# A two-layer encoder on one core: expert weights loaded as 16 KB rows for two experts at once, and the next layer's keys and values begun later, through GpSimd's DMA queue

## The chip, the cores and the metric

The kernel runs on one core of a Trainium2 chip. The metric is device time in microseconds (us), from the start of the program to its end. Engines are named as the profile names them: PE (TensorE), ACT (ScalarE), DVE (VectorE), POOL (GpSimd) and SP (SyncE, which here only issues DMAs).

## What is computed

The reference is a trunk of two layers on 512 tokens of width 1024, all in float32. Cut to what matters here:

```
for l in range(2):
    # 1) gated mixing and grouped-query attention from one projection, residual add
    # 2) cross-attention into 256 memory tokens, residual add
    mem_n = rms_norm(mem, mem_norm_g)
    kv = (mem_n @ w_kv[l])            # (256, 1024) x (1024, 2048): keys and values
    # 3) expert choice: 16 experts, each takes its 64 best tokens
    xs = h[idx]                       # (16, 64, 1024)
    a, u = xs @ w_gate[l], xs @ w_up[l]   # per expert 1024 x 1024
    y = (silu(a) * u) @ w_down[l]         # per expert 1024 x 1024
    x = x.at[idx].add(y * gates)
x = rms_norm(x, final_norm_g)
```

## The kernel before

Each layer has a dense part (steps 1 and 2) and an expert part (step 3). The dense part is many small matmuls, three for each product, since each operand is split in a high and a low half (`mm3`, L152 to L154). The expert part goes through the 16 experts in eight pairs (`experts(pr, ...)`), two experts side by side in the two halves of the array. A pair needs 24 MB of weights, for 64 rows of each expert only. Every weight is used once, so this part streams all 16 experts from HBM.

A pair has eight steps, written (pr, i). Steps (pr, 0) to (pr, 3) are gate and up: 512 hidden columns n, then half of the depth k0. Steps (pr, 4) to (pr, 7) are down, in the same way. After each step `between` calls what stands in `todo` and `plan` for it: the ranking of the next pair's tokens, its gather, its transposition and the scattered adds of the pair before. The gather (`gather`, L1188) is an indirect DMA that POOL issues at step 3 of the pair before (one step later in pair 0); its rows are 4168 bytes. PE transposes the gathered tokens at steps 5 and 6 (L1174, `turned`).

The weights are packed in HBM in the order in which they are loaded. A load (`load`, L132) brings 8 KB to each of the 128 partitions, 1 MB in all, from SP's DMA queue. The slots of 8 KB come from several pools, and `order` is a list of slot kinds that is rotated: 14 "w", two "k", two "x" and one "e". A load waits until PE has done its last matmul from the slot's old content. SP takes its loads strictly in the order in which they stand in the program.

Layer 0 has one more task: layer 1's keys and values are worked out during layer 0's expert part. `kv_start` takes slots out of the rotation for the results, for `mT` (the transposed memory tokens) and for the split weights `wkv`. The memory tokens are loaded, scaled on POOL (`mem_scaled`), and transposed on PE in four pieces (`mem_turned`, L346). Then follow eight units u: a load of 1 MB (`kv_load`), its split by ACT and DVE (`kv_split`, L143 and L144) and 48 matmuls (`kv_products`). They stand at numbered steps, `KV_FROM = 2` being pair 2: units end at steps (2, 7), (3, 3), (3, 7), ... (6, 3).

The program is built by a scheduler that may move independent instructions on an engine. Only PE keeps the written order in the down part (`te.strict`).

Of the kernel before, what the change touches and what calls it, by code (L numbers as in the profile page):

```python
# [19 lines left out]
F32 = mybir.dt.float32  # L20
F32R = mybir.dt.float32r
# [7 lines left out]
P = 128  # L29
# [62 lines left out]
def build(tc, a, out, packed):  # L92
# [10 lines left out]
    pair = pool(es, "pair", 2)  # L103
    RD, RM = 3, 14
    kvp = pool(es, "kvp", 2, side="right")
    KV_FROM = 2
    ring, more = [None], [None, None]
    order = deque()
    ps = ent(tc.tile_pool(name="ps", bufs=4, space=PSUM))
# [13 lines left out]
    def slot(shape, dt, nm, hold=False):  # L123
        kind = order.popleft() if order else "w"
        if order and not hold and kind != "y":
            order.append(kind)
        pl, tag = {"w": (ring[0], "w"), "k": (kvp, "k"), "e": (more[0], "e"), "y": (more[1], "y"), "x": (pair, "x")}[kind]
        return pl.tile(shape, dt, name=nm, tag=tag)

    def load(src, b, c):  # L130
        t = slot([P, b, c], F32, "w")
        nc.sync.dma_start(t, src)  # L132
        return t
# [188 lines left out]
    def kv_tiles():  # L322

        while "k" in order:
            order.remove("k")
        return kvp.tile([P, KD, M], F32, name="KT", tag="k"), kvp.tile([P, 2, D], F32, name="V", tag="k")
# [46 lines left out]
    class Final:  # L373
        def __init__(self):
            (a01, self.r), (b01, _) = x_stats(), x_stats()
            self.ssq = [a01[:, 0], a01[:, 1], b01[:, 0], b01[:, 1]]
            o = [slot([P, 2, D], F32, "o") for _ in range(2)]
            self.o = [o[t // 2][:, t % 2] for t in range(TT)]

        def load_gain(self):  # L380
            self.fg = slot([P, D], F32, "fg")
            nc.sync.dma_start(self.fg, a["fg"])
# [24 lines left out]
    for l in range(L):  # L407
# [3 lines left out]
        aTp[0] = pool(dense, f"aT{l}", 2)  # L411
# [401 lines left out]
        wo0 = kvp.tile([P, 4, 512], F32, name="w", tag="k")  # L813
# [37 lines left out]
        order.extend(["w"] * 7 + ["k"] + ["w"] * (RM - 8) + ["k", "w"])  # L851
# [207 lines left out]
        def wload(src, e, k0, c0, cw=512, kw=4):  # L1059
            return load(piece((*src, e), k0, kw, c0, cw), kw, cw)  # L1060

        def first_load(src, k0, c0):

            t = slot([P, 2, 2, 512], F32, "w")
# [5 lines left out]
        def second_load(src, k0, c0):  # L1070

            order.rotate(-1)
            t = again.pop(0)
            for i in range(2):
                k1 = k0 + 2 * i
                nc.sync.dma_start(t[:, i], piece(src, k1, 2, c0, 512))
            return t.rearrange("p i k c -> p (i k) c")

        again = []
# [115 lines left out]
        more[:] = ex1, eyp  # L1195
        order.extend("xxe")
        order.insert(14, "y")
# [7 lines left out]
        if l + 1 < L:  # L1205
            kv = {}

            def kv_start():
                kv["out"] = kv_tiles()
                kv["mT"] = [slot([P, KD, M], F32R, "mT", True) for _ in range(2)]  # L1210
                kv["hi"], kv["lo"] = (slot([P, KD, M], F32R, "wkv", True) for _ in range(2))
                kv["mem"] = load(mem_src, 2, D)

            def kv_load(u):
                kv["w"] = load(piece(("xattn_w_kv", l + 1), 0, KD, u * M, M), KD, M)

            def kv_split(k0):
                for k in range(k0, k0 + 4, 2):
                    split_ps(kv["w"][:, k:k + 2], kv["hi"][:, k:k + 2], kv["lo"][:, k:k + 2])

            def kv_products(u):
                mh, ml = kv["mT"]
                ac = [bank("acc") for _ in range(2)]
                for k in range(KD):
                    wh, wl = kv["hi"][:, k], kv["lo"][:, k]
                    for c in range(2):
                        if u < 4:
                            mm3(ac[c][:, 0:M], wh[:, tsl(c)], wl[:, tsl(c)], mh[:, k], ml[:, k], k == 0, k == KD - 1)
# [8 lines left out]
            step0 = 8 * KV_FROM  # L1237
            planned(step0, kv_start)
            planned(step0 + 1, lambda: mem_scaled(kv["mem"], nc.gpsimd))
            for k2 in range(KD // 2):  # L1240
                planned(step0 + 2 + k2, lambda k2: mem_turned(kv["mem"], kv["mT"], k2), k2)
            for u in range(8):
                planned(step0 + 4 + 4 * u, kv_load, u)
                planned(step0 + 5 + 4 * u, kv_split, 0)
                planned(step0 + 6 + 4 * u, kv_split, 4)
                planned(step0 + 7 + 4 * u, kv_products, u)
        carry = []

        def experts(pr, xT, hT_next, x_next):
# [106 lines left out]
            for n, (c0, cw, chunks) in enumerate(parts):  # L1356
                y = bank("acc")[:, 0:cw]
                for k0, kw in chunks:
                    if last:
                        wd = both_load(wd_, ee, k0, c0, cw, kw)  # L1360
                    else:
                        wd = [second_load((*wd_, ee[e]), k0, c0) if pr == 0 and n == 1 and k0 == 0 else
                              wload(wd_, ee[e], k0, c0, cw, kw) for e in range(2)]
# [21 lines left out]
        for pr in range(NE // 2):  # L1385
            if pr + 1 == NE // 2 and l + 1 < L:
                while "x" in order:
                    order.remove("x")
# [5 lines left out]
        order.clear()  # L1394
        mo.close()
        rst.close()
        if l + 1 < L:
            KT, V = kv["out"]
# [64 lines left out]
```

## Time and profile before

| | |
|---|---|
| device time, median of 3 | 1661.71 us (1660.9 to 1662.37) |
| device time of the profiled execution | 1661.56 us |
| its span, first to last instruction | 1659.8 us |
| PE busy | 1597.8 us, 96% of the span |
| expert part of layer 0 (first to last matmul of L1317) | 383.56 to 867.27 us |
| expert part of layer 1 | 1192.36 to 1644.6 us |
| moved by DMA | 481.89 MB, mean 290 GB/s |

The span is what the prediction counts in; 1.8 us lie around it. The two expert parts are 56% of it. Elsewhere in the span DMA is far from busy.

### The profile page before, as it was taken

Reading aid. Unit: us, or ns where it says so; the run is one execution under the profiler, and the core shown is the slowest. Engines: PE = TensorE matmul, PEld = TensorE weight load, DVE = VectorE, ACT = ScalarE, POOL = GpSimd, SP = SyncE. Lnnn points to the kernel's source line nnn. Section 1 sums busy time; section 2 is a strip of 40 time slices with the busy share of each in tenths; the row PEclk is TensorE's granted clock in tenths of the full one; section 3 lists DMA queues with packets and bytes.
Section 4 is the critical chain, followed back from the end, with each engine's and each line's share of the span. In section 5 each row is a group of like instructions: output and inputs, shape, how many; then the busy total and the mean of one; then the engine's idle time right before and its main releaser. Section 6 shows DMA issues by size and latency. Waiting matters only on the chain.

```text
span 1659.8 us, 21190 instructions
## 1 busy us (share of the span) xinstructions
PE 1597.8 (96%) x8154; PEld 933.8 (56%) x8154; DVE 779.8 (47%) x1836; ACT 511.3 (31%) x1057; POOL 105.2 (6%) x161
## 2 busy tenths in 40 slices
PE   9999999999999999999999999999999999999986
PEld 8667888875334454454448767888633333333333
DVE  5886646534425424423237866663433442332314
ACT  5776545441002111111025784454210000000002
POOL 1100000002010000000002000000300000000000
PEclk9999999999999999999999999999999999999998
DMA  6101342588998999999993102208899999999996
GB/s 223 68 26 55 124 153 77 230 337 303 420 420 359 422 420 420 421 420 420 422 376 102 51 28 100 76 26 355 305 400 420 421 420 421 420 421 421 420 422 272
DMA packets 72837, 481.89 MB, mean 290 GB/s; under 512 B 9248, under 2 KB 9632, under 8 KB 18208
## 3 DMA queue, kind: packets, MB, share of 16 engines
q1 hardware_dynamic: 67792, 468.48, 69.6%
q0 software_dynamic: 2016, 7.47, 1.1%
q10 hardware_dynamic: 2928, 4.59, 0.8%
q8 instruction: 64, 1.05, 0.3%
q14 instruction: 37, 0.30, 0.1%
HBM read 474.14 MB, written 6.37 MB: 290 GB/s over the span
## 4 chain that ended last, share of the span: by engine, by line
PE 64%; DMA 32%; DVE 1%; ACT 1%; issue 1%; POOL 0%; DVEq 0%; SPq 0%; ACTq 0%; POOLq 0%
DMA w<-i_packed 32%; PE acc L1317 19%; PE acc L152 9%; PE acc L153 9%; PE acc L154 9%; PE m L603 2%; PE m L593 2%; PE s L576 1%; PE acc L194 1%; PE s L577 1%; PE s L152 1%; PE s L153 1%; PE s L154 1%; PE m L1304 0%; PE m L870 0%
## 5 line engine op out<-in xcount | busy, mean ns | idle before, releaser
L1317 PE MATMUL acc<-w,xT 128*64 128x512 f32 x2048 | 482.8, 600 | 25.6 <-DMA w<-i_packed 25.1
L1317 PEld LDWEIGHTS acc<-w,xT 128*64 128x64 f32 x2048 | 150.3, 138 | 322.9 <-issue 274.6
L1317 PE MATMUL acc<-w,hT 128*64 128x512 f32 (+1 forms) x1088 | 243.8, 572 | 14.6 <-DVE hT L1294 12.1
L1317 PEld LDWEIGHTS acc<-w,hT 128*64 128x64 f32 x1088 | 79.7, 136 | 141.5 <-issue 110.1
L1285 ACT ACTIVATE hs<-acc,rsl 128x512 f32<-128x512 f32 x32 | 22.0, 687 | 316.4 <-PE acc L1317 271.3
L146 ACT ACTIVATE yhl<-acc,gx 128x512 fp32r<-128x512 f32 (+1 forms) x34 | 22.5, 662 | 300.3 <-PE acc L1317 300.3
L144 DVE TENSOR_TENSOR wl<-w,wh 128x512 fp32r<-128x512 f32 x96 | 66.3, 694 | 93.9 <-ACT wh L143 89.5
L147 DVE SCALAR_TENSOR_TENSOR wl<-w,cols,wh 128x512 fp32r<-128x512 f32 (+1 forms) x96 | 68.9, 727 | 62.3 <-ACT wh L146 54.5
L143 ACT ACTIVATE wh<-w 128x512 fp32r<-128x512 f32 x96 | 60.3, 631 | 106.7 <-PE acc L154 84.7
L1307 DVE TENSOR_TENSOR x<-m,x 128x512 f32<-128x512 f32 (+1 forms) x68 | 44.4, 652 | 86.7 <-PE m L1305 86.7
L146 ACT ACTIVATE wh<-w,cols 128x512 fp32r<-128x512 f32 (+1 forms) x96 | 64.8, 687 | 63.3 <-PE acc L153 37.0
L1307 DVE TENSOR_TENSOR x<-s,x 128x512 f32<-128x512 f32 (+1 forms) x68 | 44.4, 652 | 83.7 <-PE s L1305 83.7
L152 PE MATMUL acc<-wh,ah 128*128 128x512 f32 x192 | 77.8, 406 | 1.0 <-ACT wh L146 0.5
L153 PE MATMUL acc<-wl,ah 128*128 128x512 f32 x192 | 76.8, 400 | 0.6 <-DVE wl L147 0.6
L1286 DVE SCALAR_TENSOR_TENSOR hs<-acc,rsl,hs 128x512 f32<-128x512 f32 x32 | 24.0, 750 | 113.3 <-PE acc L1317 112.9
L154 PE MATMUL acc<-wh,al 128*128 128x512 f32 x192 | 77.0, 403 | 0.0
L584 ACT ACTIVATE P<-s,nb,qsc 128x512 f32<-128x512 f32 x64 | 49.8, 780 | 10.2 <-DVE nb L581 9.5
L147 DVE SCALAR_TENSOR_TENSOR yhl<-acc,gx,yhl 128x512 fp32r<-128x512 f32 (+1 forms) x34 | 24.3, 715 | 58.5 <-ACT yhl L146 58.5
L152 PE MATMUL acc<-wh,oh 128*128 128x512 f32 x128 | 51.5, 403 | 0.0
L1294 DVE COPY hT<-s 128x512 f32<-128x512 f32 x16 | 11.1, 691 | 83.6 <-PE s L1292 83.6
L154 PE MATMUL acc<-ah,wl 128*128 128x512 f32 x128 | 50.2, 392 | 0.0
L154 PE MATMUL acc<-wh,ol 128*128 128x512 f32 x128 | 50.1, 391 | 0.0
(413 smaller groups left out, 2919.2 us busy)
## 6 DMA issues: line engine op xcount, KB each, us to landing
w<-i_packed SPq DMA_DIRECT2D x426, 1024.0 KB, 19.8
w<-i_packed SPq DMA_DIRECT2D x24, 512.0 KB, 7.0
rows<-x ACTq DMA_DIRECT2D x8, 512.0 KB, 2.7
x<-i_x SPq DMA_DIRECT2D x4, 512.0 KB, 5.7
w<-i_mem SPq DMA_DIRECT2D x2, 1024.0 KB, 7.9
o_x<-o SPq DMA_DIRECT2D x4, 512.0 KB, 3.3
rp<-i_rope SPq DMA_DIRECT2D x4, 256.0 KB, 6.4
rows<-i_rows SPq DMA_DIRECT2D x2, 384.0 KB, 6.9
```

Of the source, the lines that this page charges most:

```text
L143: first = nc.scalar.activation(hi, p, AF.Copy)
L144: nc.vector.tensor_tensor(lo, p, hi.bitcast(F32), op=ALU.subtract)
L146: first = nc.scalar.activation(hi, p, AF.Copy, scale=col)
L147: nc.vector.scalar_tensor_tensor(lo, p, col, hi.bitcast(F32), op0=ALU.mult, op1=ALU.subtract)
L152: te(nc.tensor.matmul(o, lh, rh, start=start, stop=False))
L153: te(nc.tensor.matmul(o, lh, rl, start=False, stop=False))
L154: te(nc.tensor.matmul(o, ll, rh, start=False, stop=stop))
L584: last_exp[0] = nc.scalar.activation(pt, s, AF.Exp, bias=nb, scale=qsc[:, t, h:h + 1], accum_out=rs)
L593: last_turn[0] = te(nc.tensor.transpose(p[:, tsl(t)], Ps[t][:, tsl(kt)], ident))
L603: now = te(nc.tensor.matmul(pv[i * 64:(i + 1) * 64], vv[:, kt, kvh * 64:(kvh + 1) * 64], PT[kt], start=kt == 0, stop=kt == TT - 1))
L1307: nc.vector.tensor_tensor(xs_, o, xs_, op=ALU.add)
L1317: te(nc.tensor.matmul(acc[e * 64:(e + 1) * 64], lhs(k)[:, e * 64:(e + 1) * 64], ws[e], start=k == 0, stop=k == KD - 1))
```

## The change

Slots become "doubles" of 16 KB per partition, and one load of 2 MB brings the same chunk of gate, up or down for both experts of a pair. Seven "w" doubles, one "k" and one "x" rotate. Pair 0 still uses pieces of 8 KB, now as halves of doubles (`room`), and the pools "e" and "y" lend a slot for one of its loads each. Keys and values start at step 22, which is (2, 6); units end at steps (3, 7), (4, 3), ... (7, 3). The memory tokens and the eight units' weights are loaded to "e", which has left the rotation, with `nc.gpsimd.dma_start`.

```
-    RD, RM = 3, 14
-    kvp = pool(es, "kvp", 2, side="right")
-    KV_FROM = 2
+    RD, RM = 3, 7
+    kvp = pool(es, "kvp", side="right")
+    KV_STEP = 22
...
+    def double(shape, dt, nm, hold=False):
+        if hold:
+            kind = "w"
+            order.remove(kind)
+        else:
+            kind = order.popleft()
             order.append(kind)
...
-        order.extend(["w"] * 7 + ["k"] + ["w"] * (RM - 8) + ["k", "w"])
+        order.extend(["w"] * RM + ["k"])
...
-        def wload(src, e, k0, c0, cw=512, kw=4):
-            return load(piece((*src, e), k0, kw, c0, cw), kw, cw)
+        def wload(src, ee, k0, c0):
+            t = double([P, 2, 4, 512], F32, "w")
+            nc.sync.dma_start(t, piece(src, k0, 4, c0, 512, ee))
+            return [t[:, i] for i in range(2)]
...
-        more[:] = ex1, eyp
-        order.extend("xxe")
-        order.insert(14, "y")
+        ex_[0] = ex1
+        order.append("x")
+        halves.clear()
...
+            def kv_room(src, *dims):
+                t = ex1.tile([P, *dims], F32, name="w", tag="e")
+                nc.gpsimd.dma_start(t, src)
+                return t
...
-                kv["mT"] = [slot([P, KD, M], F32R, "mT", True) for _ in range(2)]
-                kv["hi"], kv["lo"] = (slot([P, KD, M], F32R, "wkv", True) for _ in range(2))
-                kv["mem"] = load(mem_src, 2, D)
+                for nm in ("mT", "wkv"):
+                    t = double([P, 2, KD, M], F32R, nm, True)
+                    kv[nm] = t[:, 0], t[:, 1]
+                kv["mem"] = kv_room(mem_src, 2, D)
...
-                kv["w"] = load(piece(("xattn_w_kv", l + 1), 0, KD, u * M, M), KD, M)
+                kv["w"] = kv_room(piece(("xattn_w_kv", l + 1), 0, KD, u * M, M), KD, M)
...
-                planned(step0 + 4 + 4 * u, kv_load, u)
-                planned(step0 + 5 + 4 * u, kv_split, 0)
-                planned(step0 + 6 + 4 * u, kv_split, 4)
-                planned(step0 + 7 + 4 * u, kv_products, u)
+                planned(KV_STEP + 6 + 4 * u, kv_load, u)
+                planned(KV_STEP + 7 + 4 * u, kv_split, 0)
+                planned(KV_STEP + 8 + 4 * u, kv_split, 4)
+                planned(KV_STEP + 9 + 4 * u, kv_products, u)
...
-                        pairs = [[wload(src, e, k0, n * 512) for src in (wg_, wu_)] for e in ee]
-                        parts = [(gi, [(k0 + i, [pairs[e][gi][:, i] for e in range(2)]) for i in range(4)])
+                        both = [wload(src, ee, k0, n * 512) for src in (wg_, wu_)]
+                        parts = [(gi, [(k0 + i, [both[gi][e][:, i] for e in range(2)]) for i in range(4)])
```

What the scheduler makes of it is seen at three places. On POOL, in pair 0 of layer 0, this stood before: the iota and the first gather (`xr<-rows`) of the expert part, then the copies from the gathered rows that wait for its landing.

```order
46 L1182 IOTA xr 128x512 [waits DMAHW7_49,PE_49]
47 L1188 DMA xr<-rows_3757,idx 128x1042 [waits DMAHW2_49,DMAHW4_49,DMAHW1_49,DMAHW6_49,DVE_49,Pool_49]
48 L1101 COPY rsl<-xr 128x1 [waits DMASW0_49]
49 L1104 COPY gx<-xr 64x1
50 L1104 COPY gx<-xr 64x1 [waits Pool_49]
```

And this stands there now. The load of the memory tokens (`i_mem`) has moved ahead of the first gather, and their scaling (L359) ahead of the copies. The load's wait on PE is for the last gate and up matmul of pair 0, from slot "e".

```order
46 L1211 IOTA xr 128x512 [waits DMAHW6_49,PE_49]
47 L1240 DMA w<-i_mem 128x2x1024 [waits DMAHW0_49,DVE_49,PE_49]
48 L1217 DMA xr<-rows_3748,idx 128x1042 [waits DMAHW3_49,DMAHW1_49,DMAHW5_49,DVE_49,Pool_49]
49 L359 TENSOR_SCALAR w<-w,rm 128x1024 [waits DMASW0_49]
50 L359 TENSOR_SCALAR w<-w,rm 128x1024
51 L1130 COPY rsl<-xr 128x1 [waits DMASW1_49]
52 L1133 COPY gx<-xr 64x1
```

On SP, this stood before around the loads issued in pair 2 of layer 0. The load w_4861 (second expert of step (2, 4)) takes the slot "e" and waits for PE's gate matmuls of step (2, 1); the five loads behind it wait for no engine.

```order
101 L132 DMA w_4859<-i_packed 128x2048 [waits DMAHW6_49]
102 L132 DMA w_4861<-i_packed 128x2048 [waits DMAHW7_49,PE_49]
103 L132 DMA w_4812<-i_packed 128x2048 [waits DMAHW0_49]
104 L132 DMA w_4814<-i_packed 128x2048 [waits DMAHW1_49]
105 L132 DMA w_4816<-i_packed 128x2048 [waits DMAHW2_49]
106 L132 DMA w_4818<-i_packed 128x2048 [waits DMAHW3_49]
107 L132 DMA w_4887<-i_packed 128x2048 [waits DMAHW4_49]
```

Now that place looks so. The load w_4996 (up of step (3, 2)) takes the double "x" and waits for PE's last down matmul of pair 2, step (2, 7). The load ahead of it, w_4863 (up of step (3, 0)), waits for the gate matmuls of step (2, 2). The four loads behind w_4996 (w_4940 and w_4942 are gate and up of step (3, 1)) wait for no engine.

```order
86 L1081 DMA w_4863<-i_packed 128x4096 [waits DMAHW7_49,PE_49]
87 L1081 DMA w_4996<-i_packed 128x4096 [waits DMAHW5_49,DMAHW0_49,PE_49]
88 L1081 DMA w_4940<-i_packed 128x4096 [waits DMAHW1_49]
89 L1081 DMA w_4942<-i_packed 128x4096 [waits DMAHW2_49]
90 L1081 DMA w_4994<-i_packed 128x4096 [waits DMAHW3_49]
91 L1081 DMA w_5041<-i_packed 128x4096 [waits DMAHW4_49]
92 L1081 DMA w_5043<-i_packed 128x4096 [waits DMAHW6_49,PE_49]
```

On POOL and DVE in pair 3 of layer 0, the first unit's weights now stand so. On POOL their load (`i_packed`) stands behind the copies that wait for the landing of pair 4's gather.

```order
65 L1217 DMA xr<-rows_3748,idx 128x1042 [waits DVE_49,Pool_49]
66 L1130 COPY rsl<-xr 128x1 [waits DMASW4_49]
67 L1133 COPY gx<-xr 64x1
68 L1133 COPY gx<-xr 64x1 [waits Pool_49]
69 L1240 DMA w<-i_packed 128x2048 [waits PE_49]
```

On DVE the first half of that unit's split (`wkv<-w`, which waits for the landing, DMASW5) stands ahead of the copy of `hT` that PE needs for step (3, 5).

```order
677 L165 SCALAR_TENSOR_TENSOR mT<-s,cols,mT 128x256 [waits Activation_49] x2
678 L162 TENSOR_TENSOR wkv<-w,wkv 128x512 [waits DMAHW1_49,DMAHW0_49,DMAHW2_49,DMASW5_49,Activation_49]
679 L162 TENSOR_TENSOR wkv<-w,wkv 128x512 [waits Activation_49]
680 L1329 COPY hT_5099<-m 128x512 [waits PE_49]
681 L162 TENSOR_TENSOR wkv<-w,wkv 128x512 [waits Activation_49] x2
```

## Rows read from the trace of the kernel before

**Rows 1.** The page: busy time, the DMA rate in 40 slices of the span, and the engines of the chain that ended last.
```profile
PE 1597.8 (96%) x8154; PEld 933.8 (56%) x8154; DVE 779.8 (47%) x1836; ACT 511.3 (31%) x1057; POOL 105.2 (6%) x161
...
GB/s 223 68 26 55 124 153 77 230 337 303 420 420 359 422 420 420 421 420 420 422 376 102 51 28 100 76 26 355 305 400 420 421 420 421 420 421 421 420 422 272
...
PE 64%; DMA 32%; DVE 1%; ACT 1%; issue 1%; POOL 0%; DVEq 0%; SPq 0%; ACTq 0%; POOLq 0%
```

**Rows 2.** Stretches of 20 us: busy time and count of each engine, granted PE clock, DMA share, GB/s. Four of layer 0's expert part, then three of layer 1's.
```profile
400.00:420.00 20.00, 20.00 (x94) 6.79 (x92) 6.66 (x20) 3.24 (x4) 0.56 (x1) 1.00 0.96 387
420.00:440.00 20.00, 19.22 (x96) 7.72 (x94) 7.21 (x13) 1.38 (x2) 1.88 (x5) 1.00 1.01 418
500.00:520.00 20.00, 20.00 (x102) 7.22 (x102) 12.08 (x38) 2.71 (x5) 1.02 (x1) 1.00 0.77 312
820.00:840.00 20.00, 16.37 (x73) 5.96 (x71) 1.67 (x3) 0.69 (x1) 0.00 (x0) 1.00 1.01 420
...
1200.00:1220.00 20.00, 20.00 (x96) 7.65 (x96) 10.06 (x34) 4.00 (x6) 1.85 (x6) 1.00 0.94 366
1220.00:1240.00 20.00, 19.22 (x98) 6.80 (x96) 4.49 (x8) 1.37 (x2) 1.60 (x2) 1.00 1.01 421
1620.00:1640.00 20.00, 19.22 (x106) 8.44 (x104) 4.68 (x7) 3.95 (x9) 0.00 (x0) 1.00 0.99 406
```

**Rows 3.** What SP's queue waited for from 478 to 512 us (us in total, times, longest).
```profile
SPq L132 <- PE acc L1317: 23.1, 4, 19.6
```

**Rows 4.** DMA share in tenths from 500 to 512 us, in slices of 0.3 us.
```profile
DMA  1411000000000000990679999999999999999999
```

**Rows 5.** PE in time order (start, us, what), a pair without keys and values: pair 2 of layer 1 and the first matmul of pair 3.
```profile
1299.29 7.04 PE L1317 MATMUL acc<-w,xT 128*64 128x512 f32 x32
...
1324.55 7.03 PE L1317 MATMUL acc<-w,xT 128*64 128x512 f32 x32
1336.39 3.65 PE L1317 MATMUL acc<-w,hT 128*64 128x512 f32 x16 [0.78 <-DVE hT L1294]
...
1350.12 2.31 PE L1317 MATMUL acc<-w,xT 128*64 128x512 f32 x10
```

**Rows 6.** PE in pairs 2 and 3 of layer 0: one piece of `mem_turned`, the last step of pair 2, gate and up of step (3, 3), the first matmul of a unit of keys and values and the next weight matmul behind the unit.
```profile
515.79 0.66 PE L346 MATMUL s<-ident,w 128*128 128x128 f32 x4
516.38 7.09 PE L1317 MATMUL acc<-w,xT 128*64 128x512 f32 x32
...
540.24 3.65 PE L1317 MATMUL acc<-w,hT 128*64 128x512 f32 x16
...
577.41 1.02 PE L1317 MATMUL acc<-w,xT 128*64 128x512 f32 x2
...
585.87 0.39 PE L152 MATMUL acc<-mT,wkv 128*128 128x256 f32 x1
...
591.80 3.65 PE L1317 MATMUL acc<-w,hT 128*64 128x512 f32 x16
```

**Rows 7.** POOL around the first gather of layer 0 (start, us, what, idle before it and what ended that), then PE at its use. The second row is DVE's, at the end of pair 0's gate and up matmuls.
```profile
418.59 0.56 POOL L1182 IOTA xr<- 128x512 f32 x1 [25.53 <-PE acc L1317]
...
420.33 0.75 DVE L1286 SCALAR_TENSOR_TENSOR hs<-acc,rsl,hs 128x512 f32<-128x512 f32 x1 [6.41 <-PE acc L1317]
...
423.74 1.17 POOL L1188 DMA_INDIRECT xr<-rows,idx  x1 [4.59 <-DVE idx L1187]
432.55 0.18 POOL L1101 COPY rsl<-xr 128x1 f32<-128x1 f32 x1 [7.65 <-DMA xr<-rows,idx]
...
434.63 0.40 PE L1305 MATMUL s<-yhl,oS 128*128 128x512 f32 x1
434.86 0.60 PE L1174 MATMUL m<-ident,xr 128*128 128x128 f32 x4
...
439.56 0.65 PE L1317 MATMUL acc<-w,xT 128*64 128x512 f32 x2
```

**Rows 8.** DMA queues (packets, MB, share of 16 engines) while the gather of Rows 7 moves (q0 is POOL's queue, q1 SP's): from 428 to 428.9 us, its first packets, and from 428 to 432 us, nearly all of it. No q0 packet lies before 428.
```profile
q1 hardware_dynamic: 32, 0.25, 68.4%
q0 software_dynamic: 29, 0.12, 33.3%
...
q1 hardware_dynamic: 154, 1.13, 69.1%
q0 software_dynamic: 142, 0.53, 33.5%
```

**Rows 9.** SP's queue alone: from 600 to 640 us, all rows of 8 KB (261 of the packets are semaphores), and from 850 to 860 us, rows of 4 KB but for a few (105 semaphores).
```profile
DMA packets 2316, 16.85 MB, mean 421 GB/s; under 512 B 261, under 2 KB 261, under 8 KB 261
q1 hardware_dynamic: 2314, 16.82, 101.1%
...
DMA packets 880, 3.75 MB, mean 375 GB/s; under 512 B 105, under 2 KB 105, under 8 KB 740
q1 hardware_dynamic: 880, 3.75, 92.6%
```

**Rows 10.** POOL at pair 4's gather (issue, and the copies at its landing), then DVE: a unit's four splits in a row and the copy of `hT`.
```profile
580.11 0.98 POOL L1188 DMA_INDIRECT xr<-rows,idx  x1 [39.10 <-DVE idx L1187]
589.49 0.18 POOL L1101 COPY rsl<-xr 128x1 f32<-128x1 f32 x1 [8.40 <-DMA xr<-rows,idx]
589.62 0.42 POOL L1104 COPY gx<-xr 64x1 f32<-64x1 f32 x2
...
590.85 2.52 DVE L144 TENSOR_TENSOR wkv<-w,wkv 128x512 fp32r<-128x512 f32 x4 [4.05 <-ACT wkv L143]
596.08 0.69 DVE L1294 COPY hT<-m 128x512 f32<-128x512 f32 x1 [2.71 <-PE m L1292]
```

**Rows 11.** The chain of waits in layer 1's expert part, its last piece before the loads take it over, by time.
```profile
1273.88 6.92 PE acc L1317 x32
...
1281.67 20.38 DMA w<-i_packed
```

**Rows 12.** PE at the end of layer 0's expert part: the last down products.
```profile
861.44 2.81 PE L1317 MATMUL acc<-w,hT 128*64 128x256 f32 x24
...
865.32 1.95 PE L1317 MATMUL acc<-w,hT 128*64 128x256 f32 x16
```

**Rows 13.** The DMA issues from 527.68 to 527.70 us: the last load of step (3, 0), its count, size and time from issue to landing.
```profile
w<-i_packed SPq DMA_DIRECT2D x1, 1024.0 KB, 21.3
```

More of the change, by code (lines that the diff above doesn't have):

```diff
@@ L121, in bank2, with room, shaped @@
         return bank("ms"[turn[0]])
-    def slot(shape, dt, nm, hold=False):
-        kind = order.popleft() if order else "w"
-        if order and not hold and kind != "y":
+    def double(shape, dt, nm, hold=False):
[4 more added lines that the diff above has]
+            kind = order.popleft()
             order.append(kind)
-        pl, tag = {"w": (ring[0], "w"), "k": (kvp, "k"), "e": (more[0], "e"), "y": (more[1], "y"), "x": (pair, "x")}[kind]
+        pl, tag = {"w": (ring[0], "w"), "k": (kvp, "k"), "x": (pair, "x")}[kind]
         return pl.tile(shape, dt, name=nm, tag=tag)
+    def room(*dims):
+        if not order:
+            return ring[0].tile([P, *dims], F32, name="w", tag="w")
+        if not halves:
+            t = double([P, 2, 2048], F32, "w")
+            halves.extend((t[:, 0], t[:, 1]))
+        return shaped(halves.pop(0), dims)
+    def shaped(v, dims):
+        v = v[:, 0:math.prod(dims)]
+        names = "abc"[:len(dims)]
+        return v.rearrange(f"p ({' '.join(names)}) -> p {' '.join(names)}", **dict(zip(names, dims)))
     def load(src, b, c):
-        t = slot([P, b, c], F32, "w")
+        t = room(b, c)
         nc.sync.dma_start(t, src)
@@ L322, in kv_tiles @@
     def kv_tiles():
[L324 removed]
+        if "k" in order:
             order.remove("k")
[L326 removed]
+        t = kvp.tile([P, 2, 2048], F32, name="KV", tag="k")
+        return shaped(t[:, 0], (KD, M)), shaped(t[:, 1], (2, D)), shaped(t[:, 0], (4, 512))
     rm = base.tile([P, 2], F32, name="rm")
@@ L376, in __init__ @@
             self.ssq = [a01[:, 0], a01[:, 1], b01[:, 0], b01[:, 1]]
-            o = [slot([P, 2, D], F32, "o") for _ in range(2)]
-            self.o = [o[t // 2][:, t % 2] for t in range(TT)]
+            o = double([P, TT, D], F32, "o")
+            self.o = [o[:, t] for t in range(TT)]
         def load_gain(self):
-            self.fg = slot([P, D], F32, "fg")
+            self.fg = room(D)
             nc.sync.dma_start(self.fg, a["fg"])
@@ L1068, in first_load, with second_load @@
             return t
-        def second_load(src, k0, c0):
+        def second_load():
             order.rotate(-1)
[L1073 to L1079, printed above, removed]
+            for e in range(2):
+                for i in range(2):
+                    nc.sync.dma_start(again[e][:, i], piece((*wd_, e), 2 * i, 2, 512, 512))
+            return [t.rearrange("p i k c -> p (i k) c") for t in again]
         def both_load(src, ee, k0, c0, cw, kw):
-            t = slot([P, 2, kw, cw], F32, "w")
+            t = room(2, kw, cw)
             nc.sync.dma_start(t, piece(src, k0, kw, c0, cw, ee))
@@ L1361, in experts @@
                     else:
-                        wd = [second_load((*wd_, ee[e]), k0, c0) if pr == 0 and n == 1 and k0 == 0 else
-                              wload(wd_, ee[e], k0, c0, cw, kw) for e in range(2)]
+                        wd = (ahead2[k0] if pr == 0 and n == 0 else second_load() if pr == 0 and k0 == 0 else
+                              wload(wd_, ee, k0, c0))
                     weights([(k, [wd[e][:, k - k0] for e in range(2)]) for k in range(k0, k0 + kw)], y,
@@ L1386, in build @@
             if pr + 1 == NE // 2 and l + 1 < L:
-                while "x" in order:
-                    order.remove("x")
+                order.remove("x")
                 hT_next, x_next = [aT_pair("a")], x_stats()
@@ L1394, in build @@
         order.clear()
+        halves.clear()
         mo.close()
@@ L1397, in build @@
         if l + 1 < L:
-            KT, V = kv["out"]
+            KT, V, wo0 = kv["out"]
     es.close()
```

37 lines of the change are left out of this document (23 added, 14 removed).

## The prediction

> **What bounds the kernel now.** The page first: PE is busy for 96% of the span, yet the chain that ended last runs 32% over weight loads [rows 1]. These are shares over stages with different limits, so the stages are read apart. In the dense parts DMA moves 23 to 155 GB/s in most slices, and only PE counts. In the expert parts DMA stands at 420 GB/s for many slices on end. The stretches of 20 us show where it does not [rows 2]: at the start of each expert part (387 and 366 GB/s, all slots full), and once in the middle of layer 0, at 500 (312). There SP stood 19.6 us at one load that waited for PE [rows 3], and DMA ran dry from 501.2 to 504.8 us, and was at full rate from about 506 [rows 4]. Afterwards it is saturated to the layer's end. In layer 1 the chain goes over to the loads at 1281.67 [rows 11] and DMA is full from 1220 to 1640 [rows 2]. So a part's end is the end of its bytes, where PE keeps up. PE's own price of a pair is 1350.12 - 1299.29 = 50.8 us [rows 5]; 24 loads at 421.2 MB per ms [rows 9] are 24 x 1.0486 / 0.4212 = 59.7 us, 2.49 each. With two units of keys and values, 591.80 - 585.87 = 5.9 us each [rows 6], PE needs 62.7 us. In layer 0's later pairs PE and DMA are level, and a wait on either one shows.
>
> **Where layer 0 restarts.** Pair 1 begins at 439.56 [rows 7]; two pairs without keys and values end at 439.6 + 2 x 50.8 - 0.4 = 540.8 us. Call this T; before, it was 543.8, since pieces of mem_turned lay in pair 2 [rows 6]. In the new order SP stands at w_4996 until T, with four loads behind it whose slots are free. This head-of-line wait is what was worth some 5 us at 500, moved and not removed. All loads up to step (3, 0) are out by then. The last of them landed at 527.7 + 21.3 = 549.0 [rows 13]; take away the old gap, 4.7 us [rows 4], and one unit's load that is no longer ahead of it, 2.5, and DMA is done with them at about 541.8, or up to 2 us later because a double is released as late as its second half. With T = 540.8 there is hardly a gap; with a later T there is one, and every us of T is a us of the layer. So nothing that DMA gains or loses before T counts in layer 0.
>
> **T itself.** POOL now issues the memory tokens ahead of the first gather, on the same queue. The old gather landed just before 432.55 and PE's add before its use ended at 434.86, so it has about 2.1 us to spare [rows 7]. The two queues share one row each, by turns: 32 packets of SP's against 29 of POOL's in the first 0.9 us, 154 against 142 in all [rows 8]. That is two on each of the 16 engines, so the turns are of one row. In busy time, rows of 4 KB move 3.75 / (10 x 0.926) = 405 MB per ms and rows of 8 KB 16.82 / (40 x 1.011) = 416 [rows 9]: a row takes 16 x 4.096 / 405 = 0.16 us and 0.315 us. Each doubling halves a row's fixed part, so after the 2.7% from 4 to 8 KB I take 1.4% from 8 to 16: about 0.62 us a row (estimate). The memory tokens are 16 rows of 4 KB per engine: 16 x (0.16 + 0.62) = 12.5 us. They are issued at about 420.3, when DVE too sees the last gate and up matmul [rows 7]. The gather's first packet came 4.4 us after its issue [rows 7, 8]; a plain load may start sooner, 2 us at least. Then the gather, 8 x (0.16 + 0.62) = 6.2 us. It lands between 420.3 + 2 + 18.7 = 441.0 and 443.4, against 434.7 at which PE wants it: PE stands 6.3 to 8.7 us; I take 7, since a plain load has no list of rows to read first. If the turns were by bytes it would be nothing. So T = 547.8, bounds 540.8 and 549.5. The Trainium skill ("DMA: Bandwidth & Descriptors", Queues, rings and completion order) has an engine drain a whole packet of 9 to 17 descriptors from one queue before it switches; rows 8 disagree, with two of each queue on every engine in 0.9 us. By its rule the order would be 8 rows of SP's, the tokens, 8 of SP's, the gather: 424.7 + 5.0 + 2.6 + 5.0 + 1.3 = 438.6, a stand of 4 us in place of 7.
>
> **After T, PE's side.** The restart: the first data come 2.3 us after T, w_4996 first although it is wanted last, then gate of (3, 1) at T + 12. PE has step (3, 0) and the add until T + 10, so it loses 3 us (0 to 5). Then the first unit. Gate and up of (3, 3) begin at T + 0.4 + 25.3 + 3 + 3 x 0.6 (three pieces of mem_turned) = T + 30.5 [rows 5, 6]. Pair 4's gather is issued 580.1 - 577.4 = 2.7 us later, lands 9.4 us behind that [rows 6, 10], and 2.4 later still beside rows of 16 KB; its copies take 0.6. Only then POOL issues the unit's weights: T + 45.6. Start 2 to 4.4, and 8 x (0.31 + 0.62) = 7.4: landed at T + 55 to 57.4. ACT's first split and two of DVE's (2.52 / 4 each) and the copy of hT, 0.7, follow [rows 10]: T + 57.5 to 60. Step (3, 5) needs that copy 1336.39 - 1324.55 = 11.8 us after (3, 3) began [rows 5], with the fourth piece T + 43. PE stands 14.5 to 17; with turns by bytes 10. I take 15. Later units load a whole unit's time ahead of use, so their loads are costed at nothing; their cover is about 31 us. The rest is work: pair 3 is 50.8 + 5.9 + 2.4 = 59.1, pairs 4 to 6 are 3 x 62.7 = 188.1, pair 7 about 50 + 5.9 (less ranking, one unit that was not there). To the last weight product: T + 0.4 + 59.1 + 188.1 + 55.9 + 3 + 15 = T + 321.5.
>
> **After T, DMA's side.** 108 loads' worth in doubles, 8 of pair 7's down, 8 units: 124 x 2.49 = 308.7 us, four gathers 5.0. Doubles gain 1.4% by rows 9; bounds 0 (a row may be cut in two on the way) and 2%. That is 54 x 4.98 x 1.4% = 3.8 us. Last landing T + 2.3 + 309.9 = T + 312.2, and the last products are 867.3 - 861.4 = 5.9 behind [rows 12]: T + 318. PE sets the end: 547.8 + 321.5 = 869.3 against 867.3, **+2.0 us** in layer 0. The slower parts of mem_scaled, SP's fewer issues and the later w_o load of the dense part hide behind PE, and are costed at nothing.
>
> **Layer 1.** No keys and values, no wait out of order on SP. About 80 doubles lie behind 1220: 80 x 4.98 x 1.4% = 5.6 us gained, bounds 0 and 8. Coarser release at the start delays saturation by half a double at most: 2 us lost. The gather beside longer rows comes 2.4 us later and PE has 2; but PE is not what ends this part. **-3.6 us.**
>
> **Sum.** 1661.56 + 2.0 - 3.6 = 1660.0 us; the profiled execution lies 0.15 under the median, so the forecast for the median is 1660.1.
>
> **The rivals.** (a) The memory tokens do not delay the gather, because the turns are by bytes or the load is early enough: T = 540.8, layer 0 at 862.3, 7 us better than the forecast: 1653. Rows 8 speak against it, but the rows of before never have two transfers in POOL's queue. (a') The two queues change turns by groups of 8 rows, as the Trainium skill's page above has it: 4 us instead of 7, so 1657. Rows 8 give it little. (b) Slower: a row of 16 KB moves no byte faster. Then layer 0 ends by DMA at T + 321.8 and, level with PE, a little above, 870; layer 1 is +2: 1666. It decides once the gain is under 0.25%. Rows 9 give a gain between 4 and 8 KB only. (c) Also slower: POOL's loads start later than a gather does. The Trainium skill ("SBUF — State Buffer", the trap box on DVE blocking DMA) says that descriptors written on GpSimd wait while DVE holds the shared port, which speaks against this queue; no row here isolates it. As a mechanism of this kernel: DVE begins its work at 420.33 too [rows 7]. Each us later at the gather and at the first unit adds a us: with 3 and 3, 1666. (d) A row of 16 KB goes as two of 8 KB: then no gain, but the gather lands at 436, 1.5 us late, and the unit's stall is 12: 1661.
>
> **Chances.** Forecast, together with (d), 0.40; (a) 0.27; (a') 0.05; (b) 0.15; (c) 0.08; other losses 0.05. What a measurement of this kernel tells from no change is about 0.2%, 3.3 us: faster 0.34 (some of the forecast's lower edge), same 0.38, slower 0.28. The forecast's own range is 1656 to 1664. With (a) and (b) and one us of their own bounds, 1651 to 1669.
>
> **What would show it.** Right: POOL's wait for the first gather ends near 442, PE's first L1205 of pair 0 stands 6 to 8 us, SP stands some 30 us at one load in pair 2 and DMA dips near 545 to 550, PE waits about 15 us for hT in pair 3, layer 1 is 3 to 4 us shorter. Wrong: two packets of SP's queue in place of one per row, a gather in time, PE waiting for loads rather than hT, or layer 1 not shorter.

## The result, and the profile after

The changed kernel takes **1671.53 us** (median; 1671.0 to 1671.61) against 1661.81: a ratio of 1.0058, 95% interval 1.0041 to 1.0076. It is 9.7 us **slower**, outside the stated range. The profiled execution takes 1671.54 us, its span is 1669.7.

The stages tell where. Layer 0's expert part, first to last weight product, went from 483.7 us (383.56 to 867.27) to 500.2 (383.09 to 883.24): +16.4. Layer 1's went from 452.2 to 447.4 (1208.03 to 1655.40): -4.9. The rest gave back 1.7.

The page after: busy time, DMA rate in 40 slices, the chain that ended last [rows 1].

```profile
PE 1575.7 (94%) x8154; PEld 923.9 (55%) x8154; DVE 781.7 (47%) x1836; ACT 513.4 (31%) x1057; POOL 110.4 (7%) x170
...
GB/s 215 73 26 52 125 127 101 195 381 306 360 425 427 315 426 414 426 426 427 426 322 177 54 26 76 77 50 241 344 372 427 427 426 426 427 428 426 426 428 288
...
PE 77%; DMA 18%; DVE 2%; ACT 1%; issue 1%; POOL 0%; SPq 0%; DVEq 0%; ACTq 0%; POOLq 0%
```

Where DMA is full it now moves 425 to 428 GB/s, not 420 to 422. The chain has moved from the loads to PE, although PE is busy for less of the span. So PE waits, and mostly for things that are not the weights. What PE waited for in layer 0's expert part (us, times, longest):

```profile
PE acc L1352 <- DVE hT L1329: 21.5, 8, 16.0
PE m L1203 <- DMA xr<-rows,idx: 9.4, 1, 9.4
PE acc L1352 <- DMA w<-i_packed: 5.1, 2, 2.6
```

The first gather, on POOL and then at PE [rows 7]:

```profile
420.10 0.96 POOL L1240 DMA_DIRECT2D w<-i_mem  x1 [1.40 <-PE acc L1352]
423.27 1.04 POOL L1217 DMA_INDIRECT xr<-rows,idx  x1 [2.21 <-DVE idx L1216]
437.17 5.69 POOL L359 TENSOR_SCALAR w<-w,rm 128x1024 f32<-128x1024 f32 x2 [12.86 <-DMA w<-i_mem]
443.88 0.19 POOL L1130 COPY rsl<-xr 128x1 f32<-128x1 f32 x1 [1.02 <-DMA xr<-rows,idx]
...
443.96 1.09 PE L1203 MATMUL m<-ident,xr 128*128 128x128 f32 x4 [9.37 <-DMA xr<-rows,idx]
444.98 5.35 PE L1352 MATMUL acc<-w,hT 128*64 128x512 f32 x16
...
450.85 1.51 PE L1352 MATMUL acc<-w,xT 128*64 128x512 f32 x6
```

The gather lands at 443.8, not 432.5, and PE stands 9.37 us. Then PE is slow (the columns are start and us): the four transpositions take 1.09 us instead of 0.60, the 16 products of a down step 5.35 instead of some 3.65. The stretches of 2 us show the reason, in the column before the DMA share, the granted clock:

```profile
436.00:438.00 2.00, 0.00 (x0) 0.00 (x0) 0.00 (x0) 0.00 (x0) 0.83 (x1) 1.00 1.04 436
...
440.00:442.00 2.00, 0.00 (x0) 0.00 (x0) 0.00 (x0) 0.00 (x0) 2.00 (x2) 0.50 1.08 450
...
446.00:448.00 2.00, 2.00 (x8) 0.58 (x6) 0.00 (x0) 0.00 (x0) 0.00 (x0) 0.50 0.08 33
448.00:450.00 2.00, 2.00 (x10) 0.42 (x6) 0.00 (x0) 0.00 (x0) 0.00 (x0) 0.89 0.00 0
450.00:452.00 2.00, 2.00 (x12) 0.91 (x12) 1.05 (x2) 0.69 (x1) 0.56 (x1) 1.00 0.54 106
```

PE did nothing from 434.6 to 443.96. The clock fell to 0.50, the level of 1.2 GHz, in this stand and was back at 1.00 (2.4 GHz) only between 448 and 450, more than 4 us after PE worked again. Pair 1 begins at 450.85 instead of 439.56. The stand costs DMA time as well: SP's next load waits for PE until 450.38, and DMA runs dry, some 5 us from 446 to 454.

SP's waits from 440 to 580 us, and stretches of 20 us (the first: SP issued w_4996 only at 552.9; the second: layer 1, DMA full):

```profile
SPq L1081 <- PE acc L1352: 107.6, 21, 17.6
SPq L1081 <- DMA w<-i_packed: 24.9, 3, 12.5
...
540.00:560.00 20.00, 20.00 (x96) 7.65 (x93) 5.18 (x8) 1.38 (x2) 1.05 (x4) 1.00 0.50 194
...
1500.00:1520.00 20.00, 15.61 (x76) 5.27 (x74) 3.05 (x6) 0.69 (x1) 0.97 (x1) 1.00 1.01 426
```

The two longest waits are both at w_4996, 12.5 us for a landing and then 17.6 for PE: the 30 us in all that the prediction named. Ten us of DMA are lost in the first stretch, against 4.7 before [rows 4]. Pair 3, on PE, POOL and DVE [rows 5, 6, 10]:

```profile
565.60 3.65 PE L1352 MATMUL acc<-w,xT 128*64 128x512 f32 x16 [2.50 <-DMA w<-i_packed]
571.82 5.08 PE L1352 MATMUL acc<-w,xT 128*64 128x512 f32 x16 [2.57 <-DMA w<-i_packed]
...
614.45 5.94 PE L1352 MATMUL acc<-w,hT 128*64 128x512 f32 x16 [16.02 <-DVE hT L1329]
...
588.88 0.96 POOL L1217 DMA_INDIRECT xr<-rows,idx  x1 [38.91 <-DVE idx L1216]
599.80 0.18 POOL L1130 COPY rsl<-xr 128x1 f32<-128x1 f32 x1 [9.96 <-DMA xr<-rows,idx]
600.28 0.58 POOL L1240 DMA_DIRECT2D w<-i_packed  x1
...
612.50 1.29 DVE L162 TENSOR_TENSOR wkv<-w,wkv 128x512 fp32r<-128x512 f32 x2 [16.19 <-ACT wkv L161]
613.72 0.68 DVE L1329 COPY hT<-m 128x512 f32<-128x512 f32 x1
```

PE waits twice for loads that SP held back, then 16.02 us for hT, which stands on DVE behind a split that waits for the unit's load, issued only at 600.28. The steps behind the second and third wait take 5.08 and 5.94 us instead of 3.65.

### The profile page after: what moved, and what is told of

The parts are those of the page before. It is cut to its first block, busy times and chain, and to the rows that moved or that the text cites. A ratio compares the mean times of both kernels' runs of the same rounds, so it can differ in the third digit from the quotient of the medians.

```text
span 1669.7 us, 20871 instructions
## 1 busy us (share of the span) xinstructions
PE 1575.7 (94%) x8154; PEld 923.9 (55%) x8154; DVE 781.7 (47%) x1836; ACT 513.4 (31%) x1057; POOL 110.4 (7%) x170
## 4 chain that ended last, share of the span: by engine, by line
PE 77%; DMA 18%; DVE 2%; ACT 1%; issue 1%; POOL 0%; SPq 0%; DVEq 0%; ACTq 0%; POOLq 0%
PE acc L1352 29%; DMA w<-i_packed 16%; PE acc L170 10%; PE acc L171 10%; PE acc L172 10%; DMA xr<-rows,idx 2%; PE m L623 2%; PE m L613 2%; PE s L596 1%; PE acc L212 1%; PE s L597 1%; PE s L170 1%; PE s L171 1%; PE s L172 1%; PE s L1339 1%
## 5 line engine op out<-in xcount | busy, mean ns | idle before, releaser
L1352 PE MATMUL acc<-w,xT 128*64 128x512 f32 x2048 | 461.9, 596 | 24.7 <-DMA w<-i_packed 24.1
L1352 PEld LDWEIGHTS acc<-w,xT 128*64 128x64 f32 x2048 | 144.0, 137 | 307.1 <-issue 267.7
L1352 PE MATMUL acc<-w,hT 128*64 128x512 f32 (+1 forms) x1088 | 239.0, 583 | 38.8 <-DVE hT L1329 25.4
L1352 PEld LDWEIGHTS acc<-w,hT 128*64 128x64 f32 x1088 | 76.2, 139 | 167.0 <-issue 126.2
L162 DVE TENSOR_TENSOR wl<-w,wh 128x512 fp32r<-128x512 f32 x88 | 60.8, 694 | 85.7 <-ACT wh L161 83.3
L161 ACT ACTIVATE wh<-w 128x512 fp32r<-128x512 f32 x88 | 55.2, 631 | 97.4 <-PE acc L172 81.0
L170 PE MATMUL acc<-wh,a 128*128 128x512 f32 x192 | 77.8, 406 | 1.0 <-ACT wh L164 0.5
L171 PE MATMUL acc<-wl,a 128*128 128x512 f32 x192 | 76.8, 400 | 0.6 <-DVE wl L165 0.6
L172 PE MATMUL acc<-wh,a 128*128 128x512 f32 x192 | 77.0, 403 | 0.0
L170 PE MATMUL acc<-wh,o 128*128 128x512 f32 x128 | 51.5, 402 | 0.0
L172 PE MATMUL acc<-wh,o 128*128 128x512 f32 x128 | 50.0, 391 | 0.0
L171 PE MATMUL acc<-wl,o 128*128 128x512 f32 x128 | 50.0, 391 | 0.0
```

Source lines behind the costliest of these rows:

```text
L161: first = nc.scalar.activation(hi, p, AF.Copy)
L162: nc.vector.tensor_tensor(lo, p, hi.bitcast(F32), op=ALU.subtract)
L170: te(nc.tensor.matmul(o, lh, rh, start=start, stop=False))
L171: te(nc.tensor.matmul(o, lh, rl, start=False, stop=False))
L172: te(nc.tensor.matmul(o, ll, rh, start=False, stop=stop))
L1352: te(nc.tensor.matmul(acc[e * 64:(e + 1) * 64], lhs(k)[:, e * 64:(e + 1) * 64], ws[e], start=k == 0, stop=k == KD - 1))
```

## The experiments

Theory A is that of the prediction, with the clock added: layer 0 lost its 16 us by three stands of PE (waits in which it does nothing) that come from the order on POOL, DVE and SP. Theory B: the late keys and values, and slots released in 16 KB, cost it. Theory C is about the gain in layer 1: not the length of a row, but fewer and larger issues. Each of the times below stands beside the kernel before on the same chip, 1661.6 to 1662.6 us.

**Memory tokens behind the gather.** One scheduling dependency (the lines that keep the two handles are left out, here and below):

```
...
+                nosync(last_d[0], last_g[0], "behind the gather")   # the memory tokens' load behind the last gather
```

> The changed kernel with one more scheduling dependency: the load of the memory tokens stands on POOL behind the gather that is written just before it (pair 3's) and no longer ahead of pair 1's. Theory A (the 16 us lost in layer 0 are stands of PE caused by the order on POOL and SP, and the lower clock behind them): the first gather lands near 433 us, PE's stand of 9.4 us in pair 0 and the half clock behind it (2.2 us) are gone, pair 1 begins near 439.5 instead of 450.9, and since SP's blocked load is released 11 us earlier the wait for loads in pair 3 shrinks from 5 us to under 2. Total 1657 us (1654 to 1661). Rival B (layer 0 is longer because a unit of keys and values now lies in pair 7 and doubles are released late): what PE gains in pair 0 is waited for later, total above 1667 us.

Measured: 1659.12 us, ratio to before 0.9987 (0.9977 to 0.9996): 12.4 us less than the changed kernel. What PE waited for:

```profile
PE acc L1354 <- DVE hT L1331: 22.7, 8, 17.2
PE acc L1354 <- DMA w<-i_packed: 4.1, 3, 2.6
PE m L1204 <- DMA xr<-rows,idx: 0.4, 1, 0.4
```

The first stand is gone (0.4) and pair 1 begins at 440.38. B falls as the main cause. The waits for loads shrank by only 1 us, though, where under 2 us in all were expected: SP still stands at w_4996, until 542.3, and the DMA share is 0.90 from 520 to 540 and 0.84 from 540 to 560.

**Splits behind the add.** The first unit's splits, one step later and behind the down product's split:

```
+                        nosync(hi, last_y[0], "behind the scatter")
+                        nosync(lows[0], last_y[1], "behind the scatter")
...
+                planned(KV_STEP + 7 + 4 * u + (u == 0), kv_split, 0, u == 0)
+                planned(KV_STEP + 8 + 4 * u, kv_split, 4, u == 0)
```

> The changed kernel, but the first unit's splits stand on ACT and DVE behind the split of pair 3's first down product, so that hT does not queue behind a load. Theory A: the stand of 16 us at step (3, 5) is gone; PE reaches the unit itself at about the time its weights land and stands there 2 to 5 us; PE gains 12 to 15 us in pair 3. DMA has been full since 555 us and its last landing (869.8) lets layer 0 end no earlier than 875.7 against 882.9, so the total gains 7 to 10 us: 1663 us (1660 to 1666). Rival B: PE is not what ends layer 0, total above 1668 us.

Measured: 1666.65 us, ratio 1.0032 (1.0019 to 1.0044), a gain of 4.9 us, less than expected. The stand moved:

```profile
PE acc L1357 <- DMA w<-i_packed: 8.3, 6, 2.6
PE m L1204 <- DVE x L1347: 6.9, 1, 6.9
PE acc L1357 <- DVE hT L1333: 6.3, 8, 0.8
```

hT costs nothing beyond its usual 0.8 each. But the splits, which still wait for the load, now hold DVE's adds of the same pair back, 6.9 us, and PE waits 3 us more for loads later. The right place was missed by one more instruction.

**SP in written order.** Each load of a double depends on the one written before it:

```
+            d = nc.sync.dma_start(t, piece(src, k0, 4, c0, 512, ee))
+            if last_w:
+                nosync(d, last_w.pop(), "in order")
+            last_w.append(d)
```

> The changed kernel with SP's loads of doubles kept in the order in which they are written, so that the load for slot x in pair 3 stands behind the three that have free slots. Theory A: no run dry of DMA at 540 to 553 us (share 0.50 in the stretch 540 to 560 becomes above 0.9), PE does not wait at step (3, 1) (5 us and 1.4 us of lower clock saved), but the two stands for POOL's transfers stay. Total 1665 us (1662 to 1668). Rival: the dry time is hidden under the later stand at (3, 5), since DMA catches up while PE stands: total within 2 us of 1671.5.

Measured: 1664.29 us, ratio 1.0015 (1.0006 to 1.0025), a gain of 7.2. The same stretch as above, and no wait of PE for a load in layer 0:

```profile
540.00:560.00 20.00, 20.00 (x95) 8.27 (x92) 5.95 (x10) 1.37 (x2) 0.77 (x3) 1.00 1.01 429
```

**Rows of 8 KB.** Each load of 2 MB becomes two:

```
+            v = piece(src, k0, 4, c0, 512, ee)
+            for i in range(2):
+                nc.sync.dma_start(t[:, i], v[:, i])
```

> The changed kernel, but each load of 2 MB issued as two of 1 MB, rows of 8 KB as before; slots, order and POOL unchanged. Theory A (rows of 16 KB move 1.5% faster, and POOL's queue gets one of its rows per row of SP's): DMA at 421 GB/s instead of 427, layer 1 loses its 5.8 us; but the memory tokens and the gather behind them move beside shorter rows, the gather lands near 437 instead of 443.8, PE stands 2 to 3 us and keeps its clock, the second stand is 3 us shorter. Total 1667 us (1663 to 1671). Rival C (the higher rate comes from 2 MB per issue, or the turns are by bytes): rate 427 stays or the first stand stays 9 us, total 1671 us or more.

Measured: 1667.32 us, ratio 1.0036 (1.0022 to 1.005). Layer 1's part is 453.2 us again, at 418 GB/s in the stretch in which the changed kernel has 426; PE's stand at the first gather falls to 2.0:

```profile
1500.00:1520.00 20.00, 16.11 (x76) 5.60 (x77) 3.74 (x7) 0.69 (x1) 1.45 (x4) 1.00 1.01 418
...
PE m L1205 <- DMA xr<-rows,idx: 2.0, 1, 2.0
```

Both halves of A's claim on rows hold: DMA moves less with the shorter row, and the longer row delays whoever takes turns with it. The edit also makes two issues of each, though, so by the rate alone C is not out; the second run with rows of 8 KB, below, tells the two apart.

**All three orders.** The first three edits together.

> The three orders together in the changed kernel: memory tokens behind pair 3's gather, the first unit's splits behind pair 3's first down product, SP's doubles in written order. Theory A: all three stands of PE in layer 0 go or shrink (first 0.4 us, wait for loads in pair 3 none, third at most 9 us with its clock), DMA is full from about 425 us on with no dry stretch, and layer 0 ends by DMA at about 859 us against 867.3 before and 882.9 in the changed kernel; layer 1 keeps 447 us against 452 before. Total 1649 us (1645 to 1654), faster than both kernels. Rival B (a late unit of keys and values, or doubles, cost layer 0 more than the stands did): total above 1658 us.

Measured: **1648.55 us**, ratio 0.9927 (0.991 to 0.9943): faster than both kernels, 13 us under before. Layer 0's part is 478.0 us, layer 1's 447.3. DMA is full from 420 to 840. What is left is the stand behind the splits, with its clock:

```profile
580.00:600.00 20.00, 11.89 (x52) 5.02 (x54) 7.04 (x12) 2.88 (x5) 2.09 (x6) 0.85 1.00 424
...
PE m L1209 <- DVE x L1353: 7.5, 1, 7.5
```

**The unit's load ahead of the gather.** SP in written order, the memory tokens behind pair 2's gather and transposed two steps earlier, and the first unit loaded two steps earlier. The splits' order is not in it; they stand where the scheduler puts them:

```
+            planned(12, kv_mem)
+            planned(KV_STEP - 2, kv_start)
...
+                planned(KV_STEP + 6 + 4 * u - 2 * (u == 0), kv_load, u)
```

> Like the kernel with all three orders, but the memory tokens are loaded behind pair 2's gather, transposed two steps earlier, and the first unit's load stands on POOL ahead of pair 4's gather, so that it lands long before hT is copied (its splits are where the scheduler puts them). Theory A: PE has no stand above 1 us in pairs 0 to 3 and keeps its clock. DMA ends layer 0 as in the kernel with all three orders, so the total is the same or up to 3 us better: 1647 us (1643 to 1652). Rival: it is PE's third stand that ends layer 0 there, and this one is 5 us or more better than that one.

Measured: 1649.27 us, ratio 0.9925 (0.9908 to 0.9941), the same time as with all three orders. No long stand is left; PE instead waits 13 times for loads, and layer 0's part is 478.0 us here too:

```profile
PE acc L1361 <- DMA w<-i_packed: 12.6, 13, 1.8
```

So with DMA full, the third stand costs nothing; it costs where DMA has lost time as well.

**Rows of 8 KB in all three orders.** As above, to see what a row is worth where DMA ends a stage.

> The kernel with all three orders, but each load of 2 MB issued as two with rows of 8 KB. Theory A (rows of 16 KB move 1.5% faster): layer 1 loses 5 us; layer 0, where PE and DMA end within a few us of each other, loses 3 to 5. Total 1657 us (1654 to 1660). Rival C (the doubles help by fewer issues and waits, not by row length): under 1651 us.

Measured: 1661.36 us, ratio 0.9995 (0.9985 to 1.0004). Layer 0's part is 483.7 us (478.0 with rows of 16 KB) and layer 1's 453.3 (447.3): 11.6 us in the two, more than expected; C would have the total under 1651. (The two totals differ by 12.8 us, but the kernel before ran 1 us longer on this run's chip.)

This edit too changes the length of a row and the number of issues together; the single packets tell which counts. From 1300 to 1400 us, with the engines full in either case, a row of 16 KB took 616 ns on average and a row of 8 KB 314 to 315, so two short rows take 12 to 13 ns more, 2%. What an issue adds on each engine, a packet of 4 bytes for its semaphore, took 9 ns: 0.36% of the engines' time with rows of 8 KB, 0.18% with 16 KB. So nearly all of the gain lies in the rows, as A has it, and the fewer issues give some 0.2%. No run changes the one without the other.

**Keys and values late in the kernel before.** `step0` is 6 more, and units two steps later still, as in the changed kernel:

```
-            step0 = 8 * KV_FROM
+            step0 = 8 * KV_FROM + 6
...
```

> The kernel before (rows and slots of 8 KB, all loads on SP) with keys and values at the steps of the changed kernel: start at step 22, units end at (3, 7) to (7, 3). Theory A: the later steps by themselves cost little, since DMA ends layer 0 there: 1662 us (1659 to 1665). Rival B: the unit in pair 7 and the fuller pairs make PE the end of layer 0: 1667 us or more.

Measured: 1667.79 us, ratio 1.0047 (1.0029 to 1.0064): 6.2 us slower, as B expected. PE at the end of pair 7's up, at the unit, and at the layer's last products [rows 12]:

```profile
844.67 2.31 PE L1317 MATMUL acc<-w,xT 128*64 128x512 f32 x8
846.91 0.38 PE L152 MATMUL acc<-wkv,mT 128*128 128x256 f32 x1
...
872.04 1.95 PE L1317 MATMUL acc<-w,hT 128*64 128x256 f32 x16
```

Pair 7 begins at 810.35 (810.01 before) and is paced by loads until its up ends at 847; then come the unit, 5.9 us, and the whole down part, 21 us, which is PE's own. Before, the down part began at 845.3 at once. So a unit in the last pair shows in full, even where DMA sets the pace. That the changed kernel pays this is not shown: behind pair 3 its PE waits for no load, so that a unit is PE's work in whichever pair it stands.

**Keys and values from ACT's queue.**

```
-                nc.gpsimd.dma_start(t, src)
+                nc.scalar.dma_start(t, src)
```

> The changed kernel with the loads of the memory tokens and of the eight units issued from ACT's queue instead of POOL's; SP's order as in the changed kernel. Theory A (the gather waits because it is second in POOL's own queue, and the first unit's load because it is issued behind POOL's wait for a landing): the first gather moves beside the memory tokens and lands at 434 to 436 us, PE stands at most 1.5 us and keeps its clock; the first unit's load is issued some 6 us earlier, so the stand for hT falls from 16 us to 7 to 10; the dry stretch of SP's order remains. Total 1656 us (1652 to 1660). Rival (any load beside 16 KB rows of SP's queue is this slow, whoever issues it): stands and total as in the changed kernel, above 1667 us.

Measured: 1657.81 us, ratio 0.9971 (0.9959 to 0.9982). PE's waits:

```profile
PE acc L1352 <- DVE hT L1329: 15.1, 8, 9.6
PE acc L1352 <- DMA w<-i_packed: 6.6, 4, 2.6
PE m L1203 <- DMA xr<-rows,idx: 2.1, 1, 2.1
```

The gather lands at 435.96, beside the memory tokens instead of behind them, and PE stands 2.1 us. The wait for hT is 6.4 us shorter, as expected of a load that does not stand behind POOL's wait. The clock still fell once: it was 0.50 from 438 to 440, and the down step behind the 2.1 us took 5.35 us, not 3.65. Behind the 2.0 us in the run with rows of 8 KB it stayed at 1.00.

**PE kept busy in its stand.** Dummy products on an unused accumulator, ahead of the transposition that waits:

```
+                    for _ in range(60):      # 38 in the second run
+                        te(nc.tensor.matmul(p[:, 0:P], ident, ident, start=True, stop=True))
```

> The changed kernel with 60 dummy matmuls of 128 columns (0.145 us each, 8.7 us in all, written to an unused accumulator) on PE just ahead of the transposition that waits for the first gather. Theory A: the half clock at 439 to 449 us follows from PE having nothing to do in its stand; with the dummies the granted clock stays at 1.0, the down step behind the stand takes 3.06 us instead of 4.8, pair 1 begins 2 us earlier, total 1669.5 us (1668 to 1671). Rival: the clock falls for another reason, step and total unchanged at 1671.5 us or later by what the dummies overrun.

Measured: 1672.74 us, ratio 1.0065 (1.0049 to 1.0082). A dummy took 0.226 us, not 0.145: the 60 products stand in the profile as 120 instructions, where a transposition is one. So they lasted 13.6 us and overran the gather by 4.4; but the clock stayed at 1.00 and the down step took 3.65 us. Hence the shorter run:

> As the run with dummy matmuls, with 38 instead of 60: at the 0.226 us that one took there they last 8.6 us and end before the gather lands. Theory A: the clock stays at 1.0, the down step behind the stand takes 3.06 us instead of 4.8 and the transposition ahead of it 0.6 instead of 1.1, total 1669.3 us (1668 to 1670.5). Rival: what the dummies save is waited for at the later stands, total 1671.5 us.

Measured: 1668.57 us, ratio 1.0043 (1.0032 to 1.0054), 3 us under the changed kernel in the median; the single times spread from 1667.38 to 1672.42, so the total alone shows little, and the trace more. PE, and the clock in the stretch that was at 0.50:

```profile
434.77 8.65 PE L1299 MATMUL acc<-ident 128*128 128x128 f32 x76
443.92 0.63 PE L1203 MATMUL m<-ident,xr 128*128 128x128 f32 x4 [0.50 <-DMA xr<-rows,idx]
444.47 3.65 PE L1356 MATMUL acc<-w,hT 128*64 128x512 f32 x16
...
446.00:448.00 2.00, 2.00 (x10) 0.43 (x6) 0.00 (x0) 0.00 (x0) 0.00 (x0) 1.00 0.21 90
```

The gather lands as late as before (POOL sees it at 443.84), and pair 1 begins at 448.65 instead of 450.85. So the lower clock came from PE's doing nothing, and its price here is 2.2 us on top of the wait.

**The kernel before, SP in written order.** The same dependency in the old kernel.

> The kernel before with its expert loads kept on SP in the order in which they are written, nothing else. Theory A: the one dry stretch of DMA in layer 0 (4.6 us at 501 to 506) is gone and layer 0 ends 4 to 5 us earlier, since DMA ends it: 1657 us (1655 to 1659). Rival: the stretch is made up for elsewhere (SP's full queue or PE): 1661.5 us.

Measured: 1657.0 us, ratio 0.9965 (0.9951 to 0.9979), 5.6 us less, as expected. The dry stretch at 500 is gone:

```profile
500.00:520.00 20.00, 20.00 (x102) 7.04 (x100) 11.32 (x36) 2.55 (x5) 1.03 (x1) 1.00 1.01 419
```

Layer 0's part is 478.8 us here, nearly the 478.0 of the changed kernel in all three orders. So of the 13 us that the latter is faster than the kernel before, SP's order alone gives 5.6 without the change; most of the rest is layer 1 (452.5 us here, 447.3 there).

## Why the prediction was wrong

The places were right, and the sizes were not. It forecast +2.0 us in layer 0 and -3.6 in layer 1; measured are +16.4 and -4.9.

**T itself: mis-sized.** The prediction took 7 us for the first stand out of bounds of 6.3 to 8.7; it is 9.37, since PE saw the gather at 443.96 instead of 443.4 at the latest, and was ready at 434.59. The choice of a lower value, "since a plain load has no list of rows to read first", was wrong: the plain load's first packet too came 4.1 us behind its issue (420.10 to 424.19), and no row shows the 2 us that the lower bound went by. A row of 16 KB took 0.616 us (0.62 estimated) and the turns were of one row. The sentence on the Trainium skill ("DMA: Bandwidth & Descriptors", Queues, rings and completion order) stands as weighed: 140 packets of SP's to 136 of POOL's in six us beside rows of 16 KB, and no stand of 4 us.

```profile
q1 hardware_dynamic: 140, 2.03, 80.7%
q0 software_dynamic: 136, 0.51, 21.4%
```

**The step that failed: a stand was priced by its wait alone.** No term of the sum held PE's clock behind a wait. It cost 2.2 us in pair 0 (0.5 in the transposition, 1.7 in the down step), 1.4 behind the waits for loads and 2.3 behind the wait for hT, where the granted clock was 0.50 too (572 to 574 and 614 to 618): 5.9 us, the largest part of the miss. The dummies confirm it at the first place; at the other two it is read from the clock and the steps alone.

**The restart.** 3 us (0 to 5) were taken; it was 5.07, plus the clock. T was 552.3 (pair 3 begins at 552.69, 0.4 behind it) instead of 547.8, and DMA ran dry for 10 us.

**The first unit.** 15 us were taken; 16.02 less the usual 0.78 is 15.2. This step holds.

**The rest of PE's work.** Pairs 4 to 6 took 189.1 us (188.1 forecast), pair 7 57.7 (55.9). From T to the end it was 330.9 us, not 321.5: 3.7 of the clock, 2.1 of the restart, 2.7 here, 0.2 of the first unit, and 0.7 in pair 3 that no row assigns.

Together: 4.5 in T (2.4 of wait, 2.2 of clock) and 9.4 behind it, 13.9 us; layer 1 and the parts outside were 2.5 better than forecast; that leaves the 11.4 us between 1660.1 and 1671.5.

**DMA's side** had an error that did not decide: its end was the last landing and 5.9 us. The late-units run shows that with a unit in pair 7 the end is up's last load, the unit and 21 us of down.

**Layer 1** was right in sign and reason (rows of 16 KB, by the two runs with 8 KB and their packets), a little larger than forecast. Of the rivals, (b) and (c), at 1666 each, came nearest in outcome, but not by their mechanisms. (b), that the row earns nothing, falls by the same runs. (c) falls because POOL's loads began no later than a gather does: their first packets came 4.1 us (memory tokens) and 3.9 us (first unit) behind the issue, a gather's 4.4 [rows 7, 8]; from ACT's queue it was 3.6. Whether DVE's work has a share in these 4 us was not tried.

## What to carry to other kernels

Where a scheduler decides the order, read the order on every queue before pricing a change: here three orderings of a few lines each turned a loss of 9.7 us into a gain of 13, of which the old kernel, too, gets 5.6 by one of them. A load put on a queue is priced by what stands behind it there, and by the turns it takes with the longest rows of other queues. A stand of PE cost its wait and, most often, slow products after it; ask also whether the stage's other bound was losing time then, because where DMA stayed full the same stand cost nothing.

## What was not expected of the hardware

- The granted clock fell to 0.50 within a stand of 9.4 us and was back at 1.00 more than 4 us after PE worked again; after a stand of 2.1 us one run showed slow products, after 2.0 us another did not, nor did the changed kernel after the first of its two waits for loads (2.50 us), but after the second (2.57). What separates these stays open.
- Rows of 16 KB moved 425 to 428 GB/s where rows of 8 KB moved 418 to 422, and were worth 11.6 us in the two expert parts of a kernel that keeps DMA full.
- A float32 product of 128 by 128 with 128 by 128 took 0.226 us back to back and stands in the profile as two instructions; four transpositions of that size, one instruction each, took 0.60.
